# Expert routing tables built mostly by VectorE and evicted with tokens innermost, and the second layer's expert sums accumulated by tokens in four PSUM banks

## The chip, the cores and the metric

The kernel runs on one core of a Trainium2 chip. The metric is the device time of one execution in microseconds. TensorE does the matrix products into PSUM, VectorE and ScalarE the elementwise work and the copies out of PSUM, SyncE issues most transfers; GpSimd has little to do here.

## The reference

A model of two blocks. The first has two layers, each a mixer (a recurrent branch and a convolution, not touched here) and then `peer`, a layer of 16,384 small experts, for 512 tokens (256 of the sequence and 256 of a context) in the first layer and 256 in the second:

```python
s = jnp.einsum('thcd,hcnd->thcn', q, p['sub_keys'])        # 8 heads, two halves, 128 keys each
s1, i1 = lax.top_k(s[:, :, 0], PEER_TOPK); s2, i2 = lax.top_k(s[:, :, 1], PEER_TOPK)   # 16 of 128
...
best, pos = lax.top_k(cand, PEER_TOPK)                     # 16 of the 256 sums s1 + s2
eidx = jnp.take_along_axis(cidx, pos, axis=-1)             # expert = 128 * i1 + i2
gw = jax.nn.softmax(best, axis=-1)
u = jnp.take(p['peer_u'], eidx, axis=0)
act = jax.nn.gelu(jnp.einsum('td,thkd->thk', hc, u), approximate=False) * gw
v = jnp.take(p['peer_v'], eidx, axis=0)
return jnp.einsum('thk,thkd->td', act, v)
```

So each token takes 8 x 16 experts, with a weight each. After the second layer comes a norm, and then a second, dense block. All inputs and outputs are float32.

## The kernel before

The kernel gathers nothing. It computes all experts densely and multiplies by a routing table that is zero where a token did not choose the expert. The experts lie on a grid of 128 x 128; "an expert" below is one of 128 groups of 128 experts. Matrix operands are split into two parts (`whi`, `wlo` and the like: one cast by ScalarE, one subtraction by VectorE), and each product is made of three matmuls.

`peer` runs in two stages. **Stage 1**, `peer_route`, with the fills: for each block `b` of 128 tokens (four in the first layer, two in the second) VectorE finds the top-k (lines 1010 to 1014 for the most part), one-hot sums turn the result into indices, transposes put them into the rows `tr`, and `peer_table` builds the table. For every token it makes a 128 x 128 matrix as a product of two one-hot matrices: `qt` (VectorE, eight tokens at a time, line 1112) and `pt`, weighted by the gate. `pt` comes from VectorE in one instruction (line 1123) or from ScalarE in two, an `Abs` and a `Relu` (lines 1120, 1121). A matmul `wps` (line 1125, two records in the trace) makes one token; four tokens share a PSUM bank, and one ScalarE copy (line 1126) evicts them into `ws`, which holds 32 tokens and goes to DRAM as `wd`. There are four `pt` buffers, so one for each token of four.

Between these pieces `fill()` calls `gelu_u` ahead of time for 64 of the 128 experts: a transfer of weights, the split (lines 238, 240), 24 matmuls `s` (line 258), a Gelu on ScalarE (line 1136) and a store (`gd`). Fills that the table has left over run after it.

**Stage 2**, `peer_experts`: for groups of four experts it loads the table's part `wt`, multiplies it with the Gelu (line 1165), splits (lines 952, 953), and `products` (line 1180) sums the four experts' outputs in PSUM, channels on the partitions, tokens on the columns: 512 columns in the first layer, 256 in the second. `done` adds each sum to `x` on VectorE (line 1226). In the last group it also squares on ScalarE (lines 320, 322) and sums the squares with a matmul `nps` (line 324) for the norm that follows.

A scheduler decides at build time in which order instructions stand in each engine's queue, from priorities in the order of the code and from what it believes things cost. On the chip every engine goes through its queue in that order.

Of the kernel before, what the change touches and what calls it, by code (L numbers as in the profile page):

```python
# [11 lines left out]
F32 = mybir.dt.float32  # L12
# [10 lines left out]
P = 128  # L23
D = 1024
KO = 8
TX = 256
# [151 lines left out]
class Core:  # L178
# [924 lines left out]
    def peer_table(self, l, b, tr, wb, pp, wd, fill):  # L1103

        nc = self.nc
        iob = self.iota.unsqueeze(1).to_broadcast([P, 8, P])
        for g in range(b * 4, b * 4 + 4):
            ws = wb.tile([P, P, 32], F32, tag="ws", name="ws")
            for t0 in range(0, 32, 8):
                c0 = g * 32 + t0  # L1110
                qt = wb.tile([P, 8, P], F32, tag="qt", name="qt")
                nc.vector.tensor_tensor(qt, iob, tr[1][:, c0:c0 + 8].unsqueeze(2).to_broadcast([P, 8, P]),
                                        op=ALU.is_equal)
                for t1 in range(0, 8, 4):
                    ps = pp.tile([P, 4, P], F32, tag="mm", name="wps")
                    for t in range(4):
                        cs = slice(c0 + t1 + t, c0 + t1 + t + 1)
                        pt = wb.tile([P, P], F32, tag="pt", name="pt", bufs=4)
                        if t % 2:
                            nc.scalar.activation(pt, self.iota, AF.Abs, bias=tr[3][:, cs])  # L1120
                            nc.scalar.activation(pt, pt, AF.Relu, bias=tr[2][:, cs], scale=tr[4][:, cs])  # L1121
                        else:
                            nc.vector.tensor_scalar(pt, self.iota, tr[0][:, cs], tr[2][:, cs], op0=ALU.is_equal,
                                                    op1=ALU.mult)
                        nc.tensor.matmul(ps[:, t, :], pt, qt[:, t1 + t], start=True, stop=True)  # L1125
                    nc.scalar.copy(ws[:, :, t0 + t1:t0 + t1 + 4].rearrange("p i t -> p t i"), ps)  # L1126
            nc.sync.dma_start(wd[g], ws)
            fill(2 if g % 4 == 1 else 1)

# [9 lines left out]
    def peer_experts(self, l, T, h2, wd, gd, ge_pool, ps_s, ps_v, done):  # L1139

        nc, tc = self.nc, self.tc
        GI = 4
        TG = T // 32
        MB = 512 // T
        NV, NA = (GI + 1, GI + 2) if T == T2 else (2 * GI, 2 * GI)
        with tc.tile_pool(name="ep", bufs=2, reuse_waits="tile") as ep:
            def operands(g):
                wt = ep.tile([P, TG, GI, 32], F32, tag="wt", name="wt")
                nc.sync.dma_start(wt, wd[:, :, g * GI:g * GI + GI, :].rearrange("g p i t -> p g i t"))
                va, aa = [], []  # L1150
                for i in range(GI):
                    e = g * GI + i
                    if e in self.stash:
                        ge = ep.tile([P, T], F32, tag="gr", name="gr", bufs=2)
                        nc.sync.dma_start(ge, gd[self.stash.index(e)])
                    else:
                        ge = self.gelu_u(l, e, T, h2, ge_pool, ps_s)
                    raw = ep.tile([P, D], F32, tag="vraw", name="vraw", bufs=3)
                    nc.sync.dma_start(raw, self.A["pev"][l, e])
                    vl = ep.tile([P, D], F32R, tag="vl", name="vl", bufs=NV)  # L1160
                    vh = ep.tile([P, D], F32R, tag="vh", name="vh", bufs=NV)
                    self.split(vh, vl, raw)
                    va.append((vh, vl))
                    gv = ge[:, :T].rearrange("p (g t) -> p g t", t=32)
                    nc.vector.tensor_mul(gv, gv, wt[:, :, i, :])
                    ah = ep.tile([P, T], F32R, tag="ah", name="ah", bufs=NA)
                    al = ep.tile([P, T], F32R, tag="al", name="al", bufs=NA)
                    self.split(ah, al, ge[:, :T])
                    aa.append((ah, al))
                return va, aa  # L1170

            def products(g, va, aa):
                for m0 in range(0, KO, MB):
                    ps = ps_v.tile([P, MB, T], F32, tag="v", name="v")
                    for m in range(MB):
                        ms = slice((m0 + m) * P, (m0 + m) * P + P)
                        n = 0
                        for i in range(GI):
                            for wi, ai in ((0, 0), (0, 1), (1, 0)):
                                nc.tensor.matmul(ps[:, m, :], va[i][wi][:, ms], aa[i][ai], start=n == 0,  # L1180
                                                 stop=n == 3 * GI - 1)
                                n += 1
                    done(m0, ps, g == P // GI - 1)
            ops = operands(0)
            for g in range(P // GI):
                nxt = operands(g + 1) if T == TX and g + 1 < P // GI else None
                products(g, *ops)
                ops = nxt or (operands(g + 1) if g + 1 < P // GI else None)

    def peer(self, l, xin, xout):  # L1190
        nc, tc = self.nc, self.tc
# [572 lines left out]
```

## Time and profile before

| | |
|---|---|
| time, median of 3 runs | 5157.22 us (5154.08 to 5162.93) |
| profiled execution | 5154.13 us; span of its instructions 5152.3 us |
| busy: TensorE, VectorE, ScalarE | 4915.5 (95%), 3428.0 (67%), 2565.2 us (50%) |
| granted TensorE clock | 0.973 over the span, 1.00 in the first layer's table and in both expert stages |
| first layer, table (four blocks of 128 tokens) | 1262 to 1667 us |
| first layer, experts | from 1738 us |
| second layer, table (two blocks) | 3774 to 3995 us |
| second layer, experts | 4012 to 4562 us |

The busy time is an average over stages with different limits, so it is read stage by stage. Matmuls overlap one another: a matmul that lasts 0.28 us may be followed by the next one 0.12 us after its start, and a TensorE that looks busy may have gaps in its work.

### The profile page before, as it was taken

The page shows a single profiled execution, that of the slowest core. Times are in us where ns is not written, and L with a number is a line of the kernel's source. Part 1 is how long each engine was busy: PE and PEld are TensorE (multiplying, and loading weights), DVE is VectorE, ACT ScalarE, POOL GpSimd, SP SyncE. Part 2 cuts the span into 40 slices and gives each one's busy share as a digit, 9 for nine tenths or more (in the row PEclk, how much of TensorE's full clock was granted, in tenths as well). Part 3 has the DMA queues.
Part 4 walks back from the last instruction along what each step waited for, and adds up shares of the span by engine and source line. Part 5 has one row for each costly group of instructions (what it writes and reads, how often), then busy time and mean ns, then how long its engine had stood idle before and what let it go on. Part 6 is the DMA issues. An engine that isn't in the chain of part 4 may idle for free.

```text
span 5152.3 us, 85900 instructions
## 1 busy us (share of the span) xinstructions
PE 4915.5 (95%) x33106; PEld 4129.6 (80%) x33106; DVE 3428.0 (67%) x7590; ACT 2565.2 (50%) x4766; POOL 246.2 (5%) x629
## 2 busy tenths in 40 slices
PE   8999998999999999999999999998999999988889
PEld 6677776778777888888887787877989999987789
DVE  4788787558994455555555566666896777764654
ACT  4345444434988322222223455555588544465564
POOL 0111111000000000000000011211000000000000
PEclk9999999999999999999999899998999999999999
DMA  4332333533444644444442332324666877734444
GB/s 139 108 96 87 90 90 106 190 123 110 167 154 181 223 147 144 142 147 140 141 146 69 106 89 73 95 63 133 195 196 215 295 224 227 226 112 124 161 131 147
DMA packets 432973, 740.48 MB, mean 144 GB/s; under 512 B 132210, under 2 KB 273202, under 8 KB 427826
## 3 DMA queue, kind: packets, MB, share of 16 engines
q1 hardware_dynamic: 431042, 732.29, 45.4%
q8 instruction: 260, 4.26, 0.3%
q10 hardware_dynamic: 1520, 2.69, 0.2%
q14 instruction: 151, 1.24, 0.1%
HBM read 622.37 MB, written 112.49 MB: 143 GB/s over the span
## 4 chain that ended last, share of the span: by engine, by line
PE 73%; ACT 12%; DVE 9%; DMA 3%; issue 2%; POOL 0%; ACTq 0%; SPq 0%; DVEq 0%; POOLq 0%
PE v L1180 20%; PE s L258 14%; PE zps L258 5%; ACT ws L1126 3%; PE adaps L279 2%; PE gtps L258 2%; PE ops L258 2%; PE qps L258 2%; ACT pt L1121 2%; PE ops L1368 2%; DVE wlo L240 2%; ACT whi L238 2%; ACT pt L1120 2%; PE yp L558 1%; PE up L582 1%
## 5 line engine op out<-in xcount | busy, mean ns | idle before, releaser
L258 PE MATMUL s<-h,whi 128*128 128x512 f32 (+1 forms) x4096 | 1059.0, 343 | 1.3 <-ACT whi L238 0.7
L240 DVE TENSOR_TENSOR wlo<-wraw,whi 128x1024 fp32r<-128x1024 f32 (+2 forms) x602 | 724.8, 1206 | 470.1 <-ACT whi L238 460.4
L238 ACT CAST whi<-wraw 128x1024 fp32r<-128x1024 f32 (+2 forms) x602 | 622.1, 1035 | 725.5 <-PE s L258 191.7
L258 PEld LDWEIGHTS s<-h,whi 128*128 128x128 f32 x4096 | 704.1, 191 | 68.8 <-ACT ge L1136 1.0
L258 PE MATMUL s<-h,wlo 128*128 128x512 f32 (+1 forms) x2048 | 704.3, 344 | 9.3 <-DVE wlo L240 9.3
L1180 PE MATMUL v<-al,vh 128*128 128x512 f32 (+1 forms) x2048 | 689.7, 337 | 0.2 <-DVE al L953 0.2
L1180 PE MATMUL v<-ah,vl 128*128 128x512 f32 (+1 forms) x2048 | 689.7, 338 | 0.0
L1180 PE MATMUL v<-ah,vh 128*128 128x512 f32 (+1 forms) x2048 | 683.2, 338 | 1.5 <-ACT ah L952 1.0
L952 ACT CAST vh<-vraw 128x1024 fp32r<-128x1024 f32 x256 | 262.3, 1050 | 725.9 <-PE v L1180 574.1
L1226 DVE SCALAR_TENSOR_TENSOR x<-v,mod,x 128x256 f32<-128x256 f32 x768 | 334.0, 478 | 280.0 <-PE v L1180 279.9
L1180 PEld LDWEIGHTS v<-ah,vh 128*128 128x128 f32 x2048 | 387.3, 190 | 49.2 <-ACT ah L952 8.7
L258 PEld LDWEIGHTS s<-h,wlo 128*128 128x128 f32 x2048 | 390.4, 191 | 44.1 <-DVE wlo L240 10.3
L1180 PEld LDWEIGHTS v<-al,vh 128*128 128x128 f32 x2048 | 388.9, 190 | 45.8 <-DVE al L953 4.3
L1180 PEld LDWEIGHTS v<-ah,vl 128*128 128x128 f32 x2048 | 388.2, 190 | 40.6 <-issue 1.4
L953 DVE TENSOR_TENSOR vl<-vraw,vh 128x1024 fp32r<-128x1024 f32 x256 | 308.8, 1221 | 104.4 <-ACT vh L952 104.1
L258 PE MATMUL zps<-h,whi 128*128 128x512 f32 (+3 forms) x896 | 292.8, 404 | 18.9 <-DVE lz L363 7.5
L1125 PEld LDWEIGHTS wps<-qt,pt 128*128 128x128 f32 x1536 | 215.9, 190 | 109.5 <-ACT pt L1121 91.3
L1125 PE MATMUL wps<-qt,pt 128*128 128x128 f32 x1536 | 272.5, 292 | 22.1 <-ACT pt L1121 13.7
L258 PEld LDWEIGHTS zps<-h,whi 128*128 128x128 f32 (+1 forms) x896 | 167.6, 196 | 60.1 <-issue 19.4
L1126 ACT COPY ws<-wps 128x512 f32<-128x512 f32 x192 | 210.4, 1096 | 5.7 <-PE wps L1125 5.2
L279 PE MATMUL adaps<-adaw,cs 128*2 128x128 f32 x1536 | 205.7, 274 | 5.8 <-DMA adaw<-ada 4.4
L1121 ACT ACTIVATE pt<-pt,tr,tr 128x128 f32<-128x128 f32 x384 | 180.3, 489 | 2.5
(613 smaller groups left out, 9545.6 us busy)
## 6 DMA issues: line engine op xcount, KB each, us to landing
wraw<-peu SPq DMA_DIRECT2D x256, 512.0 KB, 4.0
vraw<-pev SPq DMA_DIRECT2D x256, 512.0 KB, 4.5
wraw<-win SPq DMA_DIRECT2D x139, 512.0 KB, 3.5
adaw<-ada SPq DMA_DIRECT2D x96, 512.0 KB, 3.6
wd<-ws SPq DMA_DIRECT2D x24, 2048.0 KB, 6.7
wt<-wd SPq DMA_DIRECT2D x32, 1024.0 KB, 6.8
wraw<-w_q SPq DMA_DIRECT2D x32, 512.0 KB, 3.7
gd<-ge SPq DMA_DIRECT2D x64, 256.0 KB, 2.3
```

What stands on the lines that cost most here:

```text
L238: nc.scalar.copy(hi, raw)
L240: nc.vector.tensor_sub(lo, raw, hi.bitcast(F32))
L258: nc.tensor.matmul(out, w[wi][:, k, :], a[ai][:, k, ts], start=n == 0, stop=n == 3 * ko - 1)
L279: nc.tensor.matmul(ps[0:2, i * P:i * P + P], self.cs[:, k, :], w[:, k, :], start=k == 0, stop=k == KO - 1)
L952: self.nc.scalar.copy(hi, src)
L953: self.nc.vector.tensor_sub(lo, src, hi.bitcast(F32))
L1120: nc.scalar.activation(pt, self.iota, AF.Abs, bias=tr[3][:, cs])
L1121: nc.scalar.activation(pt, pt, AF.Relu, bias=tr[2][:, cs], scale=tr[4][:, cs])
L1125: nc.tensor.matmul(ps[:, t, :], pt, qt[:, t1 + t], start=True, stop=True)
L1126: nc.scalar.copy(ws[:, :, t0 + t1:t0 + t1 + 4].rearrange("p i t -> p t i"), ps)
L1180: nc.tensor.matmul(ps[:, m, :], va[i][wi][:, ms], aa[i][ai], start=n == 0, stop=n == 3 * GI - 1)
L1226: nc.vector.scalar_tensor_tensor(x[:, k, ts], src[:, m, ts], self.mod[l][:, 40 + k, s:s + 1], x[:, k, ts], op0=ALU.mult, op1=ALU.add)
```

## The change

In `peer_table` ScalarE makes `pt` for one token of four instead of two, VectorE for three. The eviction's access patterns are turned: before it read PSUM in order and wrote each element 128 bytes from the last, now it reads four tokens 512 bytes apart and writes them next to each other. In the second layer (`T == TX`) `products_t` replaces `products`: the tokens' weighted activations are the stationary operand, 512 channels of the expert's output matrix the moving one, and the sums over all 128 experts stay in four PSUM banks (128 tokens x 512 channels each). At the end `channels` copies them out, transposes them 128 x 128 at a time, and hands them to `done`, which now runs once.

```diff
                     for t in range(4):
                         cs = slice(c0 + t1 + t, c0 + t1 + t + 1)
                         pt = wb.tile([P, P], F32, tag="pt", name="pt", bufs=4)
-                        if t % 2:
+                        if t == 3:
                             nc.scalar.activation(pt, self.iota, AF.Abs, bias=tr[3][:, cs])
                             nc.scalar.activation(pt, pt, AF.Relu, bias=tr[2][:, cs], scale=tr[4][:, cs])
                         else:
                             nc.vector.tensor_scalar(pt, self.iota, tr[0][:, cs], tr[2][:, cs], op0=ALU.is_equal,
                                                     op1=ALU.mult)
                         nc.tensor.matmul(ps[:, t, :], pt, qt[:, t1 + t], start=True, stop=True)
-                    nc.scalar.copy(ws[:, :, t0 + t1:t0 + t1 + 4].rearrange("p i t -> p t i"), ps)
+                    nc.scalar.copy(ws[:, :, t0 + t1:t0 + t1 + 4], ps.rearrange("p t i -> p i t"))
...
+            def products_t(g, va, aa):
+
+                for i in range(GI):
+                    for b in range(2):
+                        bs = slice(b * P, b * P + P)
+                        for n, (wi, ai) in enumerate(((0, 0), (1, 0), (0, 1))):
+                            for c in range(2):
+                                nc.tensor.matmul(acc[b][c], aa[i][ai][:, bs], va[i][wi][:, c * 512:c * 512 + 512],
+                                                 start=g + i + n == 0, stop=g == P // GI - 1 and i == GI - 1 and n == 2)
+
+            def channels():
+
+                rows = []
+                for b in range(2):
+                    r = ep.tile([P, D], F32, tag="vraw", name="vrow", bufs=3)
+                    for c in range(2):
+                        (nc.scalar.copy, nc.vector.tensor_copy)[c](r[:, c * 512:c * 512 + 512], acc[b][c])
+                    rows.append(r)
+                for m0 in range(0, KO, 2):
+                    ps = ps_s.tile([P, 2, T], F32, tag="s", name="vt")
+                    for m in range(2):
+                        for b in range(2):
+                            nc.tensor.transpose(ps[:, m, b * P:b * P + P], rows[b][:, (m0 + m) * P:(m0 + m) * P + P],
+                                                self.ident)
+                    done(m0, ps, True)
+            if T == TX:
+                acc = [[ps_v.tile([P, 512], F32, tag="v", name="acc") for c in range(2)] for b in range(2)]
+                products = products_t
```

The order in which the instructions stand changes in three regions alone: the two tables, and the second layer's expert stage.

ScalarE's queue in the last table block of the first layer (`L1120` is the `Abs`, `L1121` the `Relu`, `L1126` the eviction, `L1136` a fill's Gelu). Before:

```order
L1121 ACTIVATE pt<-pt,tr_9729,tr_9731 128x128
L1120 ACTIVATE pt<-iota,tr_9730 128x128
L1126 COPY ws<-wps 128x4x128
L1121 ACTIVATE pt<-pt,tr_9729,tr_9731 128x128
L1120 ACTIVATE pt<-iota,tr_9730 128x128
L1136 ACTIVATE ge<-s 128x512
L1121 ACTIVATE pt<-pt,tr_9729,tr_9731 128x128
L1120 ACTIVATE pt<-iota,tr_9730 128x128 x2
L1126 COPY ws<-wps 128x4x128
L1121 ACTIVATE pt<-pt,tr_9729,tr_9731 128x128 x2
```

and now, the same region:

```order
L1120 ACTIVATE pt<-iota,tr_9730 128x128
L1121 ACTIVATE pt<-pt,tr_9729,tr_9731 128x128
L1120 ACTIVATE pt<-iota,tr_9730 128x128
L1121 ACTIVATE pt<-pt,tr_9729,tr_9731 128x128
L1126 COPY ws<-wps 128x128x4
L1120 ACTIVATE pt<-iota,tr_9730 128x128
L1126 COPY ws<-wps 128x128x4
L1121 ACTIVATE pt<-pt,tr_9729,tr_9731 128x128
L1126 COPY ws<-wps 128x128x4
L1120 ACTIVATE pt<-iota,tr_9730 128x128
L1121 ACTIVATE pt<-pt,tr_9729,tr_9731 128x128
```

There is one `Abs` and one `Relu` to an eviction instead of two of each. The first eviction shown belongs to the quad of the first `Relu`, the second to that of the second `Relu`, the third to that of the `Relu` just ahead of it.

VectorE's queue in the same block (`L1123` makes a `pt`, `L1112` eight tokens of `qt`, `L240` is a fill's split). Before:

```order
L1123 TENSOR_SCALAR pt<-iota,tr_9727,tr_9729 128x128 x5
L1112 TENSOR_TENSOR qt<-iota,tr_9728 128x1024
L1123 TENSOR_SCALAR pt<-iota,tr_9727,tr_9729 128x128
L240 TENSOR_TENSOR wlo<-wraw,whi 128x1024
L1123 TENSOR_SCALAR pt<-iota,tr_9727,tr_9729 128x128 x2
L1112 TENSOR_TENSOR qt<-iota,tr_9728 128x1024
```

and now:

```order
L1123 TENSOR_SCALAR pt<-iota,tr_9727,tr_9729 128x128 x6
L1112 TENSOR_TENSOR qt<-iota,tr_9728 128x1024
L1123 TENSOR_SCALAR pt<-iota,tr_9727,tr_9729 128x128 x3
L240 TENSOR_TENSOR wlo<-wraw,whi 128x1024
L1123 TENSOR_SCALAR pt<-iota,tr_9727,tr_9729 128x128 x3
L1112 TENSOR_TENSOR qt<-iota,tr_9728 128x1024
```

Six instead of four `pt` stand to a `qt`. In this block 113 matmuls `s` now stand on TensorE between the table's matmuls instead of 188.

TensorE's queue at the end of the second layer's experts (`nps` is the norm, `pps` the dense block that follows). Before:

```order
L1180 MATMUL v<-ah,vh 128x256
L1180 MATMUL v<-al,vh 128x256
L1180 MATMUL v<-ah,vl 128x256
L324 MATMUL nps<-nsq,onesd 128x256 x4
L258 MATMUL pps<-hh_44317,whi 128x256 x2
```

and now:

```order
L1192 MATMUL acc<-vh,ah 128x512 x2
L1192 MATMUL acc<-vl,ah 128x512 x2
L1192 MATMUL acc<-vh,al 128x512 x2
L1207 MATMUL vt<-ident,vrow 128x128 x12
L324 MATMUL nps<-nsq,onesd 128x256 x12
L1207 MATMUL vt<-ident,vrow 128x128 x4
L324 MATMUL nps<-nsq,onesd 128x256 x4
```

Before, three more such groups of four `nps` stood among the last products; now all sixteen stand behind the last one, and the last four transposes behind twelve of them.

## Rows read from the trace of the kernel before

**Rows 1.** Windows: length, then busy us of each engine with its instructions, clock, DMA.

```profile
1262.00:1582.00 320.00, 309.41 (x1618) 236.86 (x1617) 278.55 (x762) 283.72 (x566) 0.00 (x0) 1.00 0.46 165
1582.00:1667.00 85.00, 83.11 (x449) 61.17 (x448) 45.33 (x84) 82.82 (x171) 0.00 (x0) 1.00 0.44 155
...
3774.00:3902.00 128.00, 121.95 (x962) 114.96 (x961) 109.96 (x227) 114.27 (x225) 0.00 (x0) 1.00 0.65 221
3902.00:3995.00 93.00, 88.72 (x673) 80.93 (x672) 55.40 (x93) 91.73 (x190) 0.00 (x0) 1.00 0.58 197
...
4012.00:4562.00 550.00, 548.34 (x4536) 546.06 (x4534) 413.63 (x697) 255.21 (x387) 1.50 (x1) 1.00 0.71 228
```

**Rows 2.** Windows of tile `s` alone: PE, PEld, DVE, ACT as above.

```profile
1262.00:1667.00 405.00, 310.77 (x1032) 178.28 (x1031) 0.00 (x0) 25.32 (x43) 1.00 0.46 163
1582.00:1667.00 85.00, 61.65 (x193) 32.00 (x192) 0.00 (x0) 4.68 (x8) 1.00 0.44 155
3774.00:3995.00 221.00, 168.59 (x1117) 142.75 (x1116) 0.00 (x0) 17.71 (x47) 1.00 0.62 211
```

**Rows 3.** Waits, 1582 to 1667: who, for whom, us in total, times, longest.

```profile
DVE pt L1123 <- PE wps L1125: 25.8, 34, 1.6
PEld wps L1125 <- ACT pt L1121: 16.8, 46, 0.7
```

**Rows 4.** Groups of instructions: count, busy us, mean ns, idle before.

```profile
L1126 ACT COPY ws<-wps 128x512 f32<-128x512 f32 x192 | 210.4, 1096 | 5.7 <-PE wps L1125 5.2
...
L1042 ACT COPY q<-qps 128x512 f32<-128x512 f32 x16 | 9.3, 581 | 0.0
```

**Rows 5.** Timeline in the first layer's tables: start, duration, instruction, idle before.

```profile
1405.92 0.60 DVE L1123 TENSOR_SCALAR pt<-iota,tr,tr 128x128 f32<-128x128 f32 x2
...
1407.30 0.87 ACT L1121 ACTIVATE pt<-pt,tr,tr 128x128 f32<-128x128 f32 x2
...
1408.07 0.39 ACT L1120 ACTIVATE pt<-iota,tr 128x128 f32<-128x128 f32 x1
...
1408.36 1.09 ACT L1126 COPY ws<-wps 128x512 f32<-128x512 f32 x1
1408.39 0.86 PE L1125 MATMUL wps<-qt,pt 128*128 128x128 f32 x6
...
1409.01 0.70 PE L258 MATMUL s<-h,whi 128*128 128x512 f32 x2
...
1665.61 0.39 ACT L1120 ACTIVATE pt<-iota,tr 128x128 f32<-128x128 f32 x1
1666.03 0.49 ACT L1121 ACTIVATE pt<-pt,tr,tr 128x128 f32<-128x128 f32 x1
1667.10 1.11 ACT L1126 COPY ws<-wps 128x512 f32<-128x512 f32 x1 [0.58 <-PE wps L1125]
1667.98 1.08 ACT L238 CAST whi<-wraw 128x1024 fp32r<-128x1024 f32 x1
```

**Rows 6.** Timeline of TensorE in both expert stages: 11th product after, 10th after.

```profile
4152.44 0.28 PE L1180 MATMUL v<-ah,vh 128*128 128x256 f32 x1
...
4153.76 0.28 PE L1180 MATMUL v<-ah,vl 128*128 128x256 f32 x1
2149.65 0.39 PE L1180 MATMUL v<-ah,vh 128*128 128x512 f32 x1
...
2151.91 0.39 PE L1180 MATMUL v<-al,vh 128*128 128x512 f32 x1
```

**Rows 7.** Timeline of TensorE at the second expert stage's end.

```profile
4548.19 1.99 PE L324 MATMUL nps<-nsq,onesd 128*128 128x256 f32 x8
4549.83 0.47 PE L1180 MATMUL v<-ah,vh 128*128 128x256 f32 x1
...
4561.30 0.28 PE L1180 MATMUL v<-ah,vl 128*128 128x256 f32 x1
4562.66 2.00 PE L324 MATMUL nps<-nsq,onesd 128*128 128x256 f32 x8 [1.09 <-ACT nsq L320]
```

More of the change, by code (lines that the diff above doesn't have):

```diff
@@ L1188, in peer_experts @@
                 ops = nxt or (operands(g + 1) if g + 1 < P // GI else None)
+            if T == TX:
+                channels()
     def peer(self, l, xin, xout):
```

## Prediction, made before the changed kernel ran

> **What bounds the kernel now.** I read the windows view first, cut at the places that the change touches. TensorE is busy 95 to 100% of each stretch [rows 1], but matmuls are pipelined, so I set the busy time against the work: counted records times their start-to-start time. A 512-column product follows the last one after 2.26/10 = 0.226 us, a 256-column one after 1.32/11 = 0.120 us [rows 6], and a table product (each `wps` matmul runs as two records) after 0.62/6 = 0.103 us per record [rows 5].
>
> - Second expert stage, 4012 to 4562: back to back, nothing waited for. TensorE is the bound and every nanosecond saved there is kept.
> - Last table block of layer 1, 1582 to 1667: TensorE's work is 193 x 0.226 + 256 x 0.103 = 70 of 85 us [rows 2]. ScalarE is busy 82.8 of 85, VectorE 45.3 [rows 1]; TensorE's longest waits end on `pt` of ScalarE (16.8 us), and VectorE waits 25.8 us for TensorE to hand `pt` buffers back [rows 3]. ScalarE is the bound. Layer 2's second block is alike, 91.7 of 93 us [rows 1].
> - First three blocks of layer 1, 1262 to 1582: VectorE 278.6, ScalarE 283.7 of 320 [rows 1], since VectorE also does the next block's top-k. Nearly balanced. Layer 2's first block, 110 and 114 of 128, likewise.
>
> Expert products `s` that the tables leave over run behind them at 0.226 or 0.120 us apiece. So what a table gains is gained only as TensorE's idle time inside it; leftover work is paid later.
>
> **Edit 1, one token in four on ScalarE.** ScalarE's price of four tokens before, start to start: two `Abs` at 0.29, two `Relu` at 0.385, the eviction 0.88 [rows 5], together 2.23. 32 quads make 71.4 us, and the remaining 11.4 of the 82.8 us are 8 fills (193/24), 1.4 each. After, by throughput: 0.29 + 0.385 + 0.88 = 1.56 a quad. But the order shows what throughput hides. Before, an `Abs` or a fill mostly stood between a `Relu` and the eviction that needs it. After, the eviction often stands right behind its own `Relu`, and ScalarE must wait out the way over TensorE: 1.07 us from `Relu`'s start to the eviction's, while `Abs` to `Relu` takes 0.42 (the last four rows of [rows 5]). The four `pt` buffers also make the next `Abs` wait for the same way. Walking the pattern of four quads in the order shown (Abs, Relu, Abs, Relu, evict, Abs, evict, Relu, evict, Abs, Relu, evict): 0, 0.42, 1.49, 1.91, 2.31, 3.19, 3.48, 4.36, 5.43, 6.31, 6.73, 7.80, and the next starts at 8.68. That is 2.17 us a quad with today's eviction: little won.
>
> **Edit 2, the eviction.** So its price decides. Today it reads PSUM in one run and writes SBUF in steps of 128 bytes: 1.096 us, against 0.581 for the copy of the same size without steps [rows 4]. After, it writes runs of four neighbours but reads PSUM in steps of 512 bytes, which no row shows. Bounds from the rows: 0.581 (start to start 0.38) and 1.096 (0.88); a dearer one is a rival. The write, the side that was stepped, is then packed by fours, so I put it nearer the row without steps: 0.8 us, 0.60 start to start. The same walk gives 7.63 per four quads, 1.91 each.
>
> Last block of layer 1: 32 x 1.91 = 61 plus some 4 us of fills that don't fit into the waits = 65, against 85: 20 less (12 less at 0.88, 27 less at the lower bound, where TensorE's 53 us of work and VectorE's 45 + 8 are the floor). But in the built order 365 instead of 316 `s` products are left over: 49 x 0.226 = 11 back.
> First three blocks: VectorE gets 96 more `pt`. One costs 0.34 alone, two take 0.60 [rows 5], so 0.26 to 0.34 each: 25 to 33 us on 278.6, 304 to 311. Of the 41 us that VectorE idled, I let 7 a block stay for the waits inside the table: 325 to 332 instead of 320, I take +6. The ends are 312 (-8) and 340 (+20).
> Layer 1 together: -20 + 11 + 6 = **-3** (-25 to +20).
>
> Layer 2, second block: 32 x 1.91 = 61, plus 14 fills of which half fit into waits, some 12: 73 against 93, -20; in the built order 84 products fewer stand inside and are paid later at 0.120: +10. First block: VectorE's 110 + 8 to 11, with some idle time, fills its 128 us; 0. **-10** (-16 to +3).
>
> **Edit 3, expert sums by tokens.** 3072 products of 256 columns become 1536 of 512, the columns are the same: 3072 x 0.120 = 368.6 against 1536 x 0.226 = 347.1, **-21.5**; the saving is the 14 ns by which two narrow products outlast a wide one, 1536 times. The 512-column rows are layer 1's, with the operands' roles swapped; both are full 128 x 128 loads, so I carry the price over. The VectorE updates that go bought nothing: it is busy 413.6 of 550 us there [rows 1] and isn't waited for.
> [...]
>
> New tail. Before, the norm of two channels stood in the stream of products three times, 1.64 us and a step of some 0.1 each, and its last part ended 3.4 us after the last product (4561.30 to 4564.66) [rows 7]. After, from the last product's start X: copies done at X+0.9 (0.3 as from `wps` to its eviction, 0.58 of copying), transposes and first update X+2.1, then twelve norm products, 0.41 apiece (8 records in 1.64 us), to X+7.5. The fourth group of transposes stands **behind** these twelve in TensorE's queue: its update and squares X+8.7, norm end about X+11.2. So 7.8 more at the end, 3 x 1.75 less inside: +2.5 (0 to +4). Experts: -21.5 + 2.5 = **-19** (-23 to -12).
>
> **Sum.** -3 - 10 - 19 = -32. The profiled execution took 5154.1 us (span 5152.3), 3 below the median of the runs; 5154 - 32 = **5122 us**. Ahead of the first table, between layer 1's experts and the second table, and behind the norm all instructions stand in the same order as before, so nothing else should move.
>
> **Rivals.**
> 1. The eviction stays at about 1.1 us. Layer 1's last block saves 12, layer 2's 12, the three blocks get longer by 10: layer 1 +9, layer 2 0, experts -19: 5144. For it: stepping nearly doubles the price in the one row there is. 0.18.
> 2. The other side: the stepped PSUM read is dearer than today's stepped write. ScalarE's chain runs through the eviction once a quad, in 64 quads where ScalarE binds and in half of the other 128: 13 us for every 0.1 us above 0.88. The 10 us left of rival 1 are used up at 0.96; slower by 0.2% from 1.04 start to start (about 1.26 us); at 1.5 it is 5225. For it: nothing measured; against: steps cost at most half a microsecond in the row there is. [...] 0.10.
> 3. Both tables run at TensorE's pace: idle falls from 405 - 1032 x 0.226 - 1024 x 0.103 = 66 to some 30 us in layer 1, in layer 2 from 221 - 1117 x 0.120 - 512 x 0.103 = 34 to 15 [rows 2]: -36 - 19 - 19, 5080. Against: the order's waits above. 0.10.
> 4. VectorE becomes the bound for good: 340 us in the three blocks, +20 - 12 + 11 in layer 1, -3 in layer 2, -19: 5151. 0.07.
> 5. [...] 0.05. [...]
>
> **Chances and range.** Forecast 0.50, its own range 5108 to 5134. For 8 in 10 the range goes from 5098 to 5153: it holds the forecast and rivals 1, 4 and 5, and leaves out 2 and 3. A difference of 0.2%, 10 us, is about what a measurement of this kernel can tell. Faster by more: forecast, 3, 5 and six tenths of 1, 0.76; same: the rest of 1, and 4, 0.14; slower: 2, 0.10.
>
> **What would show it.** Eviction: the mean of the `ws` copies, and whether ScalarE sits idle before them, waiting for `wps`. Last block of layer 1: some 65 us, ScalarE no longer 97% busy. Three blocks: VectorE above 90% busy. Experts: `acc` products 0.226 us apart and the stage some 531 us long; transposes twelve, then norms, then four. Wrong if the eviction costs more than 1.2 us, if `acc` products, which change PSUM bank each time, are not 0.226 apart, or if the three blocks take more than 340 us.

## The result, and the profile after

The changed kernel takes **5098.02 us** (median of 4 runs, 5095.33 to 5101.27) against 5155.65 for the kernel before (4 runs): ratio 0.9886, 95% interval 0.9869 to 0.9903. It is faster by 57.6 us where 32 were forecast, and lies at the very edge of the range. The profiled execution has a span of 5099.5 us, 52.9 less than before.

The windows view of the changed kernel, cut at the same places as [rows 1]: layer 1's first three blocks, its last block, layer 2's two blocks, layer 2's sums.

```profile
1263.90:1569.30 305.40, 300.03 (x1654) 249.94 (x1653) 300.32 (x862) 193.28 (x377) 0.00 (x0) 0.99 0.48 177
1569.30:1627.00 57.70, 57.70 (x366) 49.61 (x365) 47.76 (x112) 48.01 (x105) 0.00 (x0) 1.00 0.46 178
...
3741.80:3861.70 119.90, 118.23 (x959) 114.59 (x958) 116.54 (x259) 82.88 (x159) 0.00 (x0) 1.00 0.67 234
3861.70:3936.00 74.30, 74.15 (x596) 71.17 (x595) 58.59 (x122) 59.12 (x122) 0.00 (x0) 1.00 0.61 226
...
3959.00:4490.00 531.00, 527.46 (x3003) 466.34 (x3002) 320.38 (x440) 258.76 (x377) 2.03 (x2) 0.99 0.70 233
```

ScalarE, the fourth busy column, binds nowhere now: 193 of 305 us, 48 of 58. In the first three blocks VectorE is the busiest, with 300 of 305; whether it also sets their length is taken up in experiment 7. The groups view says why ScalarE is free; this is the eviction, with count, busy time, mean ns, and ScalarE's idle time before it:

```profile
L1126 ACT COPY ws<-wps 128x512 f32<-128x512 f32 x192 | 111.3, 580 | 48.7 <-PE wps L1125 45.9
```

It costs 0.580 us where it cost 1.096, and the copy without steps costs 0.581 [rows 4]. The idle time before it rose from 5.7 to 48.7 us: the wait behind its own `Relu` is there as the prediction had it, but on an engine with time to spare. The waits view of the last block has no long wait left (compare [rows 3]):

```profile
ACT ws L1126 <- PE wps L1125: 7.8, 13, 0.7
DVE pt L1123 <- PE wps L1125: 3.8, 11, 0.5
PEld wps L1125 <- ACT pt L1121: 2.8, 9, 0.3
```

TensorE's timeline in layer 2's sums shows two products per row, 0.45 to 0.46 us from row to row, so some 0.227 apiece, close to the 0.226 of the 512-column rows of [rows 6]:

```profile
4155.65 0.61 PE L1192 MATMUL acc<-vh,ah 128*128 128x512 f32 x2
4156.11 0.62 PE L1192 MATMUL acc<-vl,ah 128*128 128x512 f32 x2
4156.56 0.62 PE L1192 MATMUL acc<-vh,al 128*128 128x512 f32 x2
```

And the end of that stage, which answers to [rows 7]: the last product at 4489.79, twelve transposes, twelve norm products of two records, four transposes, four norm products, and then nothing until the dense block.

```profile
4490.02 1.81 PE L1207 MATMUL vt<-ident,vrow 128*128 128x128 f32 x12
...
4492.20 5.45 PE L324 MATMUL nps<-nsq,onesd 128*128 128x256 f32 x24 [0.37 <-ACT nsq L320]
...
4497.48 0.60 PE L1207 MATMUL vt<-ident,vrow 128*128 128x128 f32 x4
...
4499.11 1.99 PE L324 MATMUL nps<-nsq,onesd 128*128 128x256 f32 x8 [1.03 <-ACT nsq L320]
```

**Stages of all kernels.** Lengths in us, from first and last instructions in each trace: a block from its first `wps` to the next block's, the last block of a layer to the end of its last eviction; "left over" from there to the first expert product.

| | before | changed | again | sums alone | split alone | eviction alone | both table edits | split by place | no split |
|---|---|---|---|---|---|---|---|---|---|
| L1, three blocks | 320.4 | 304.1 | 303.8 | 320.5 | 331.5 | 294.2 | 304.0 | 294.3 | 294.3 |
| L1, last block | 85.7 | 58.9 | 58.9 | 85.7 | 69.2 | 76.0 | 58.9 | 62.0 | 76.0 |
| L1, left over | 70.4 | 82.0 | 82.0 | 70.3 | 81.5 | 70.9 | 82.0 | 85.1 | 70.9 |
| **L1 table, sum** | 476.5 | 445.0 | 444.7 | 476.5 | 482.2 | 441.1 | 444.8 | 441.4 | 441.1 |
| L2 table, left over with it | 237.8 | 217.4 | 217.3 | 237.8 | 234.2 | 216.9 | 217.4 | 216.7 | 218.7 |
| L2, sums | 549.3 | 530.7 | 528.8 | 526.2 | 554.6 | 550.0 | 554.7 | 526.0 | 523.5 |
| last product to dense block | 14.2 | 22.3 | 22.4 | 22.3 | 14.2 | 14.2 | 14.2 | 19.9 | 19.8 |
| dense block | 576.8 | 587.4 | 575.4 | 574.8 | 584.7 | 576.0 | 575.1 | 578.6 | 574.8 |

The parts of layer 1's table that kernels share repeat to a few tenths of a microsecond. Layer 2's sums do not (530.7, 528.8 and, with the same products in experiment 5, 526.0), nor does the dense block, which is a finding of its own.

### The profile page after: what moved, and what is told of

It reads as the page before. It is cut to its first block, busy times and chain, and to the rows that moved or that the text cites. A ratio compares the mean times of both kernels' runs of the same rounds, so it can differ in the third digit from the quotient of the medians.

```text
span 5099.5 us, 82466 instructions
## 1 busy us (share of the span) xinstructions
PE 4872.8 (96%) x31586; PEld 4065.7 (80%) x31586; DVE 3377.8 (66%) x7536; ACT 2388.0 (47%) x4384; POOL 246.9 (5%) x629
## 4 chain that ended last, share of the span: by engine, by line
PE 81%; DVE 9%; ACT 4%; DMA 4%; issue 1%; POOL 0%; SPq 0%; ACTq 0%; DVEq 0%; POOLq 0%
PE s L258 18%; PE v L1180 14%; PE acc L1192 6%; PE zps L258 5%; PE wps L1125 4%; PE adaps L279 3%; PE qps L258 2%; PE ops L258 2%; PE gtps L258 2%; PE ops L1399 2%; DVE wlo L240 2%; PE yp L558 1%; PE up L582 1%; PE zp L587 1%; PE zbps L258 1%
## 5 line engine op out<-in xcount | busy, mean ns | idle before, releaser
L240 DVE TENSOR_TENSOR wlo<-wraw,whi 128x1024 fp32r<-128x1024 f32 (+2 forms) x602 | 725.6, 1207 | 476.4 <-ACT whi L238 460.5
L1180 PE MATMUL v<-ah,vl 128*128 128x512 f32 x1024 | 401.3, 392 | 0.0
L1180 PE MATMUL v<-al,vh 128*128 128x512 f32 x1024 | 400.3, 391 | 0.0
L1180 PE MATMUL v<-ah,vh 128*128 128x512 f32 x1024 | 393.1, 391 | 0.5
L1257 DVE SCALAR_TENSOR_TENSOR x<-v,mod,x 128x256 f32<-128x256 f32 x512 | 220.0, 478 | 204.1 <-PE v L1180 204.1
L1125 PE MATMUL wps<-qt,pt 128*128 128x128 f32 x1536 | 229.6, 285 | 1.4 <-ACT pt L1121 0.6
L1180 PEld LDWEIGHTS v<-ah,vh 128*128 128x128 f32 x1024 | 191.0, 188 | 47.7 <-ACT ah L952 7.3
L1180 PEld LDWEIGHTS v<-al,vh 128*128 128x128 f32 x1024 | 192.2, 188 | 45.3 <-DVE al L953 4.0
L1180 PEld LDWEIGHTS v<-ah,vl 128*128 128x128 f32 x1024 | 192.2, 188 | 40.5 <-issue 1.4
L258 PEld LDWEIGHTS zps<-h,whi 128*128 128x128 f32 (+1 forms) x896 | 169.9, 198 | 60.8 <-issue 19.9
L258 PE MATMUL zps<-h,wlo 128*128 128x512 f32 (+3 forms) x448 | 179.2, 401 | 0.9 <-DVE wlo L240 0.9
L572 POOL COPY krp<-kr 64x128 f32<-64x128 f32 (+1 forms) x448 | 152.3, 340 | 549.2 <-PE yp L558 309.7
```

The costliest lines, as they stand in the source:

```text
L240: nc.vector.tensor_sub(lo, raw, hi.bitcast(F32))
L258: nc.tensor.matmul(out, w[wi][:, k, :], a[ai][:, k, ts], start=n == 0, stop=n == 3 * ko - 1)
L572: nc.gpsimd.tensor_copy(krp[hs, 0:n, hh], KR[d][hs, 0:n, c * 64:c * 64 + 64])
L1257: nc.vector.scalar_tensor_tensor(x[:, k, ts], src[:, m, ts], self.mod[l][:, 40 + k, s:s + 1], x[:, k, ts], op0=ALU.mult, op1=ALU.add)
```

## The experiments

**1. The sums alone.** The changed kernel with both table lines set back:

```diff
-                        if t == 3:
+                        if t % 2:
...
-                    nc.scalar.copy(ws[:, :, t0 + t1:t0 + t1 + 4], ps.rearrange("p t i -> p i t"))
+                    nc.scalar.copy(ws[:, :, t0 + t1:t0 + t1 + 4].rearrange("p i t -> p t i"), ps)
```

> The second layer's expert sums by tokens alone; both tables as before. First table to experts 476 us and second table to experts 297, as before. From the second layer's first expert product to the last: 549 less 1536 x 0.014 less three pauses of 1.75, 523 us; from the last product to the dense block 8 more than before (22 instead of 14). Theory 'the tail cools TensorE': the dense block behind it again takes 10 us more than before (587 instead of 577), so the time falls by 8 only, to about 5148. Theory 'each kernel meets the clock's falls at its own places': the dense block takes anything from 575 to 590, and the granted clock falls in another stretch of it; 5137 to 5150.

Measured: 5135.9 us, ratio 0.9959 (0.9945 to 0.9973). The sums took 526.2, 3 more than expected, and the way to the dense block 22.3. But the dense block took 574.8 us behind this longer tail: "the tail cools TensorE" fell. The other theory's bounds, 575 us for that block and 5137 for the whole, were missed by 0.2 and 1.1 us.

**2. The split alone.** The kernel before with `if t == 3:` in place of `if t % 2:`.

> One token in four on ScalarE, eviction as before, experts as before. Theory 'the eviction's price decides' (the walk of the prediction at 0.88 start to start gives 2.17 us a quad against 2.23 before, less what fits into waits): the last block of layer 1 takes 73 to 83 us instead of 85, the first three together 320 to 330 instead of 320, the time within 10 us of before. Theory 'the fewer activations decide' (throughput 1.56 a quad): last block 61, first three 305, layer 2's second block 70, the time 40 us below before.

Measured: 5164.0 us, ratio 1.0017 (1.0004 to 1.0030): no gain, if anything a loss. The three blocks took 331.5 us, 11.1 more than before, of which 26 more `s` products in them (867 instead of 841) make 5.9. The last block took 69.2 us, between what the two theories had, 73 to 83 and 61; of its 16.5 us less, 75 fewer `s` products (119 instead of 194) account for 17.0. Its windows (three blocks, last block):

```profile
1263.90:1595.40 331.50, 306.74 (x1646) 247.36 (x1645) 303.48 (x860) 225.97 (x375) 0.00 (x0) 1.00 0.46 163
1595.40:1664.60 69.20, 62.25 (x376) 50.54 (x375) 49.05 (x113) 60.74 (x107) 0.00 (x0) 1.00 0.41 151
```

and its waits in the three blocks, where TensorE waits for `pt` of ScalarE although ScalarE is busy only 226 of 331 us, and ScalarE for `wps`:

```profile
PEld wps L1125 <- ACT pt L1121: 45.9, 77, 1.0
ACT ws L1126 <- PE wps L1125: 25.0, 44, 1.3
PE wps L1125 <- ACT pt L1121: 19.6, 61, 0.5
```

That is the chain of the prediction's walk (an eviction of 1.1 us that waits behind its own `Relu`, and holds up the next `Abs`): a latency, which fewer activations did not shorten here.

**3. The eviction alone.** The kernel before with

```diff
-                    nc.scalar.copy(ws[:, :, t0 + t1:t0 + t1 + 4].rearrange("p i t -> p t i"), ps)
+                    nc.scalar.copy(ws[:, :, t0 + t1:t0 + t1 + 4], ps.rearrange("p t i -> p i t"))
```

> The eviction with tokens innermost alone; two tokens in four on ScalarE as before, experts as before. Theory 'the eviction's price decides': 0.58 us instead of 1.10, so ScalarE's quad is 2.23 - 0.50 = 1.73 us: last block of layer 1 some 69 us instead of 85, layer 2's second block 77 instead of 93; in the first three blocks VectorE keeps its 279 us of work, ScalarE falls to 234, and they take 290 to 300 instead of 320. Time 35 to 50 us below before. Theory 'the split decides': 10 us or less below before.

Measured: 5099.09 us, ratio 0.9901 (0.9880 to 0.9922). One line gives as much as the whole change, 57 us where 35 to 50 were expected; "the split decides" fell. Its eviction, and its windows (three blocks, last block):

```profile
L1126 ACT COPY ws<-wps 128x512 f32<-128x512 f32 x192 | 111.4, 580 | 10.4 <-PE wps L1125 7.7
```

```profile
1257.70:1551.90 294.20, 290.47 (x1619) 242.88 (x1618) 273.34 (x762) 249.98 (x566) 0.00 (x0) 1.00 0.50 179
1551.90:1627.90 76.00, 76.00 (x449) 63.27 (x448) 45.05 (x84) 73.10 (x172) 0.00 (x0) 1.00 0.49 174
```

The last block takes 7 us more than the 69 expected, though ScalarE works only 73 of 76: TensorE's work there, 192 products and 256 table products, is 69.8. Layer 2's second block was missed by as much (84.1 us, 77 expected).

**4. Both edits of the table.** The kernel before with the lines of 2 and 3.

> Both edits of the table, experts as before. First table to experts 445 us as in the changed kernel, second table to experts 275. Layer 2's experts 549 + 7 for the 58 products left over. Theory 'the parts add up': the time is before - 31 - 22 + 7 = 5109, and the dense block takes its 577 us, since the tail ahead of it is that of before. Theory 'each kernel meets the clock's falls at its own places': the dense block differs from 577 by more than 3 us, either way.

Measured: 5108.83 us, ratio 0.9911 (0.9895 to 0.9928), as added up. (The 275 us expected from the second table to the experts is not the stage of the table above, which has 217.4; the step from 297 to 275 is 22 us, the measured one 20.4.) Beside the eviction alone, the split makes the layer 1 table 3.7 us longer and layer 2's table with its sums 5.3 (217.4 + 554.7 against 216.9 + 550.0), against 9.7 between the medians, whose intervals overlap. The 3.7 us repeat: 444.7 to 445.3 in every kernel with both edits, 441.1 in experiments 3 and 9. The 5.3 are hardly more than the 4.7 by which layer 2's sums of the same products differ between executions. So behind a cheap eviction the split costs time in layer 1; for layer 2 that is not shown.

**5. The tail.** The changed kernel, with one group of transposes in a bank of the sums, which are free by then:

```diff
-                    ps = ps_s.tile([P, 2, T], F32, tag="s", name="vt")
+                    pool, tag = (ps_v, "v") if m0 == 6 else (ps_s, "s")
+                    ps = pool.tile([P, 2, T], F32, tag=tag, name="vt")
```

> The changed kernel, with the fourth group of transposes in a bank of the sums that the copies have freed, so that it need not stand behind the first twelve norm products. From the last product of the second layer's sums to the dense block: 22.27 us in the changed kernel. Theory 'the queue position of the fourth group costs': its update and squares no longer follow the twelve norm products, the norm is then paced by ScalarE's 16 pairs of squares at 0.41 us, and the stretch is 1.5 to 2 us shorter, 20.5. Theory 'the squares pace it anyway': under 0.5 us shorter. Everything ahead as in the changed kernel within 2 us.

Measured: 5079.67 us in one run, 19.86 us from the last product to the dense block, 2.4 less. All sixteen transposes now stand together, and the norm products run through:

```profile
4483.98 2.14 PE L1208 MATMUL vt<-ident,vrow 128*128 128x128 f32 x16
4486.17 7.17 PE L324 MATMUL nps<-nsq,onesd 128*128 128x256 f32 x32
```

The queue position did cost. The rest of the difference to 5098 is not the tail: the dense block (574.3) and the sums (526.0) were also shorter in this execution.

**6. Runs of two tokens.** The changed kernel, with its eviction in another order of writing:

```diff
-                    nc.scalar.copy(ws[:, :, t0 + t1:t0 + t1 + 4], ps.rearrange("p t i -> p i t"))
+                    nc.scalar.copy(ws[:, :, t0 + t1:t0 + t1 + 4].rearrange("p i (a t) -> p a i t", a=2), ps.rearrange("p (a t) i -> p a i t", a=2))
```

> The changed kernel, but its eviction writes runs of two tokens (8 bytes) instead of four (16 bytes): same 512 elements, same stepped read of PSUM. Measured so far: runs of one (4 bytes), PSUM read in one run, 1.096 us; runs of four, PSUM read stepped, 0.580; contiguous copy of the same size 0.581. [...] Theory 'anything below 16 bytes is slow': 1.1 us, last block 69 us.

Measured: 5109.42 us in one run, the stages of the table as in the changed kernel (three blocks 303.9, last block 59.1). The eviction:

```profile
L1126 ACT COPY ws<-wps 128x512 f32<-128x512 f32 x192 | 119.2, 621 | 47.7 <-PE wps L1125 45.6
```

So for the same 512 elements: runs of 4 bytes 1.096 us, of 8 bytes 0.621, of 16 bytes 0.580, no steps 0.581. "Anything below 16 bytes is slow" (1.1) fell. So does an even price for every run: by estimate, drawn from 512 runs at 1.096 us and 128 at 0.580, it puts these 256 at 0.75. The step from 4 to 8 bytes took off 0.475 us, that from 8 to 16 another 0.041; what makes the difference is not shown. The stepped read of PSUM, the fear of rival 2, costs nothing that these rows show (0.580 against 0.581).

**7. The split by place.** Two tokens in four on ScalarE, but one in layer 1's last block, with the sums and the tail of 5:

```diff
-                        if t == 3:
+                        if t == 3 or (t == 1 and (l or b < 3)):
```

> Eviction with tokens innermost, expert sums by tokens, the fourth group of transposes in a freed bank, and the split by place: two tokens in four on ScalarE, except in the last table block of layer 1, one in four. By adding the stages measured: first three blocks of layer 1 294 us (as with the eviction alone; 304 in the changed kernel), last block 59, first table to experts 436 (445 in the changed kernel), second table to experts 217, sums 527, tail 20.5. Time 15 to 20 below the changed kernel if the dense block takes the same 587 us there, about 5079; 5067 if it takes 575. Theory 'VectorE is the bound of the three blocks once the eviction is cheap': those 294 us. Theory 'TensorE or the chain over it is': the three blocks stay at 304.

Measured: 5076.54 us, ratio 0.9854 (0.9837 to 0.9870). The three blocks took 294.3 (VectorE has 273.6 us of work there instead of 300.3), the length that goes with "VectorE is the bound". Block by block the rows don't show such a bound. These are the third blocks of the changed kernel and of experiment 3, whose table there is that of this one:

```profile
1468.80:1568.00 99.20, 97.07 (x541) 81.33 (x540) 97.85 (x270) 61.85 (x122) 0.00 (x0) 1.00 0.49 178
1452.60:1551.90 99.30, 98.20 (x548) 82.07 (x547) 79.50 (x179) 83.59 (x190) 0.00 (x0) 1.00 0.51 180
```

Both take 99 us, with VectorE (the third busy column) at 97.9 or 79.5. All of the gain is in the second block, 110.7 to 100.3 us, where VectorE is busy nearly throughout in both but 33 fewer `s` products stand now. Over the three blocks 26 fewer products (841 instead of 867) make 5.9 of the 9.8 us; TensorE's idle time, counted as in the prediction, falls only from 29.1 to 25.1.

Nor does the table as a whole gain by it. It took 441.4, not 436: the last block's order left 63 more `s` products than experiment 3's to be paid behind it, 63 x 0.226 = 14.2 us, and they took what the shorter block (62.0 instead of 76.0) had given.

**8. The changed kernel again**, unaltered.

> The changed kernel once more, unaltered, for one question: is the fall of the granted clock 127 us into the dense block (0.50 for 18 us while TensorE is busy, with 10 us lost) a property of this kernel, or of one execution? Theory 'of the kernel': the dense block takes 587 us again with the fall in the same place. Theory 'of the execution': 575 to 578 us in some profiles and 587 in others. All stages ahead of it within 1 us of the first profile, the time 5095 to 5102.

Measured: 5095.15 us in one run; every stage from the first table to the end of layer 1's experts within half a microsecond, the mixer between the layers 980.3 instead of 973.8, the dense block 575.4 instead of 587.4. So it is of the execution, not of the kernel. The windows view over one and the same stretch of work, cut at the same instructions, first in the first profile of the changed kernel, then in this one (the last column but two is the granted clock):

```profile
4639.00:4668.00 29.00, 29.00 (x211) 23.90 (x208) 7.11 (x16) 7.53 (x18) 0.96 (x1) 0.71 0.22 69
```

```profile
4641.74:4663.74 22.00, 22.00 (x212) 18.18 (x208) 7.05 (x16) 7.55 (x18) 0.96 (x1) 1.00 0.32 91
```

29 us at a mean clock of 0.71 against 22 at 1.00. From 4640 to 4656 it was 0.50, from 4657 to the end of the stretch 1.00. In the 45 us ahead of the stretch TensorE was busy 40.3 us at a mean of 0.92, in it throughout; products of 32 to 64 columns alternate there with some of 256.

**9. No split.** As 7, with `if t % 2:` as in the kernel before, so that only the eviction, the sums and the tail differ from it.

> The changed kernel with the split of before everywhere (two tokens in four on ScalarE) and the fourth group of transposes in a freed bank; it differs from the last kernel only in the last table block of layer 1. There the eviction alone gave 75.9 + 70.9 us (block and products left over), the split by place 62.0 + 85.1. Theory 'behind a cheap eviction both tables go at TensorE's pace, and what a faster block leaves out is paid behind it': first table to experts 441 us as in both, the time that of the split by place within 3 us, 5074 to 5080. Theory 'the split is worth something where ScalarE binds': first table to experts 445 or more, the time 5 to 10 us above the split by place.

Measured: 5077.15 us, ratio 0.9846 (0.9827 to 0.9865), layer 1's table 441.1 us. It equals the split by place, so "worth something where ScalarE binds" fell. Its whole interval lies below that of the changed kernel, 0.9869 to 0.9903: it beats both kernels.

**10. Eight `pt` buffers.** As 9, with

```diff
-                        pt = wb.tile([P, P], F32, tag="pt", name="pt", bufs=4)
+                        pt = wb.tile([P, P], F32, tag="pt", name="pt", bufs=8)
```

> The kernel beside it with eight pt buffers instead of four. Of layer 1's first three blocks some 25 of 294 us are TensorE's idle time (294 less 841 products at 0.226 and 768 table products at 0.103). Theory 'pt comes late because its buffers come free late': with eight, VectorE and ScalarE run ahead, and the three blocks take 275 to 288 us. Theory 'VectorE's sum of work binds them' (it is busy 194 of the first two blocks' 195 us): the first two blocks stay at 94.6 and 100.3; only the third, where VectorE is busy 79.5 of 99.3, can shrink.

Measured: 5144.06 us in one run, layer 1's table 479.5, as long as before the change: the three blocks 103.4, 105.0 and 67.8, the last 113.6. Neither theory holds as it was put, since the scheduler answered the buffers with another order: `s` products left the first three blocks (673 instead of 841) for the last one (289 instead of 192). The waits view of that last block shows the engines handing work round in turn:

```profile
DVE wlo L240 <- ACT whi L238: 42.2, 9, 5.8
ACT whi L238 <- PE s L258: 27.4, 7, 4.0
DVE qt L1112 <- PE wps L1125: 19.4, 13, 2.3
```

Whether late buffers cost anything in the order with four is left open.

## Why the prediction was wrong

The direction was right, but the case that came is not the forecast's. By its own steps, in the profiled execution:

- **Layer 1's table: -3 forecast (-25 to +20), -31.5 measured.** This is the step that failed. *First three blocks*: +6 forecast, -16.3 measured. The sentence "Of the 41 us that VectorE idled, I let 7 a block stay for the waits inside the table" priced the 96 more `pt` and gave the cheaper eviction nothing, in blocks where ScalarE was busy 283.7 of 320 us [rows 1]. Taken apart, the split costs +11.1 there (331.5, inside the 325 to 332 of the prediction), the eviction gives 26.2 (294.2), both together 16.3. VectorE's work was sized well (300.3 and 303.5 against 304 to 311), but of its idle time, of which the prediction kept 21 us, 5 remain. That idle time was no fixed cost of the table: before the change VectorE waited 14.7 us for ScalarE's casts and 19.4 for `pt` buffers that TensorE hands back, and TensorE waited 53.2 us for ScalarE's `pt`, of which 13.4 are left (rows under this list). *Last block*: -20 forecast, -26.8 measured; *left over*: +11 and +11.6.
- **The eviction: 0.8 us chosen, 0.580 measured**, the lower of the two bounds. From its start to the next instruction it was not the 0.38 of the lower bound but 0.46 to 0.48. No row shows that 0.38: the unstepped copy has 0.48 in the trace of before, as the first two timeline rows under this list show. The walk through the queue came close at either price, without the fills that the prediction added to it: for the old eviction it gave 2.17 us a quad, 69.4 in 32, and experiment 2 measured 69.2; walked once more at 0.47 it gives 7.24 for four quads, 1.81 each, 57.9 in 32, against 58.9. The second agreement proves little, since TensorE's work in that block, 52.8 us, with 6 of idle time gives it too, and the block of experiment 7, with the same table work on ScalarE and 12 more `s` products (2.7 us), took 62.0.
- **Layer 2's table: -10 (-16 to +3), -17.2 measured**: -7.8 in the first block, where I had put 0 (the same omission), -20.6 in the second (forecast -20), +11.2 for 93 more products behind it (1656 instead of 1563, at 0.120; +10).
- **The sums: -19 (-23 to -12), -13.7 measured**: 18.6 less up to the last product and 8.0 more behind it, and 3.2 of the 93 products just named, which ran inside this stage, taken out. The wide product saves what [rows 6] promised: experiment 1's stage is 23.1 us shorter, of a forecast 21.5 for the products and 5.25 for the three pauses that go. The 3.6 us that are missing are nearly all one pause of TensorE early in the stage, from 4044.0 to 4047.3. The changed kernel has it too: 3.9 us for `whi`, in the waits from 3959 to 3980 shown under this list, where ScalarE waits for late weights ahead of it; just behind it the granted clock is 0.50, from 3971 to 3977. In experiment 5, with the same products, the pause was 1.6 us and the stage 4.7 us shorter; in experiment 9, with the products of experiment 1, it was 2.0 and the stage 25.8 us shorter than before. Rival 5, with 0.05 of the chances, had the wide product save far less than 21.5 us, from a price that no run shows; the runs show 0.227 us for a wide product where two narrow ones took 0.240 [rows 6], and the 23.1 us of experiment 1. It is out.

- **The tail: +7.8 at the end forecast, +8.0 measured**, by the position of the fourth group that the order showed; experiment 5 takes 2.4 of it back.
- **"Nothing else should move"**: +9.5 in the profiled execution, of which the dense block +10.6. Experiment 8 shows that this belongs to the execution. Without these 9.5 us the profiled execution would have taken 5091.8 us, below the range: that the time comes as near as it does is luck.

Waits in layer 1's first three blocks before (1262 to 1582), and the first of them in the changed kernel (1263.9 to 1569.3):

```profile
PEld wps L1125 <- ACT pt L1121: 53.2, 132, 1.0
DVE pt L1123 <- PE wps L1125: 19.4, 43, 1.6
DVE wlo L240 <- ACT whi L238: 14.7, 11, 4.2
...
PEld wps L1125 <- ACT pt L1121: 13.4, 47, 0.3
```

The timeline of the kernel before, a copy without steps and the instruction right behind it, and that of the changed kernel, the eviction and the instruction right behind it:

```profile
1126.42 0.58 ACT L1042 COPY q<-qps 128x512 f32<-128x512 f32 x1
1126.90 0.77 ACT L1034 COPY sc<-sps 128x128 f32<-128x128 f32 x4
...
1590.80 0.57 ACT L1126 COPY ws<-wps 128x512 f32<-128x512 f32 x1
...
1591.26 0.40 ACT L1120 ACTIVATE pt<-iota,tr 128x128 f32<-128x128 f32 x1
```

Its waits at the start of layer 2's sums, 3959 to 3980:

```profile
PEld s L258 <- ACT whi L238: 3.9, 1, 3.9
DVE vl L953 <- ACT vh L952: 3.9, 5, 2.4
ACT vh L952 <- DMA vraw<-pev: 3.8, 3, 2.8
```

**The rivals.** Rival 3, TensorE's pace, priced at 5080 with a chance of 0.10, is the one that came nearest: TensorE's idle time by the same formula is 363.0 - 984 x 0.226 - 1024 x 0.103 = 35 us in layer 1 (rival: some 30, before: 66) and 194.3 - 1036 x 0.120 - 52.7 = 17 in layer 2 (rival: 15, before: 34). I held the order's waits against it; they exist (48.7 us before the evictions), but with the eviction at 0.58 they no longer end last. Block by block of layer 1 that idle time is 15 to 20 us with the dear eviction (the kernel before, experiment 2) and 6 to 12 with the cheap one (the changed kernel, experiments 3 and 7), whichever engine makes `pt`. Rival 1, the dear eviction, is what experiment 2 measures: layer 1's table +5.7 where it had +9. Rival 2 had the wrong sign of the risk: the stepped read of PSUM was free (0.580 us against 0.581). Rival 4 had VectorE busy throughout the three blocks, and it is, 300 of 305 us, but at 305 and not 340, and by the third block of experiment 7 it is not shown to be their bound.

**The edit named first was worth nothing.** Of the 57.6 us, the eviction and the sums give all; the split takes 3.7 back in layer 1's table, and 7.6 of the whole when it stands alone. A block that it shortens hands `s` products to the stretches beside it. The parts do not add up to the whole: both table edits (47.6) and the sums (20.5) make 68.1 us. The profiled execution lost 10.6 in the dense block, but experiment 8, which did not, took 5095.15 us against the median of 5098.02, so where the 10 us go is open.

## What to carry to other kernels

Two edits to one chain are not priced one after the other: a cheaper eviction paid as much where another engine looked as busy (7.5 to 9.5 us in each of the first three blocks) as where ScalarE alone did (9.7 in the last), because the other engine's idle time was waiting, directly or by way of TensorE, for ScalarE. Where a stage's filler work is paid later at TensorE's pace, ask what TensorE waits for and not who is busiest, and try each edit alone before keeping the set. Compare kernels stage by stage when single stages differ by 10 us from one execution to the next, as the dense block did here (587.4 and 575.4).

## What the hardware showed that was not expected

- Of three run lengths, a ScalarE copy with a stepped write paid dearly only for runs of one 4-byte element: 1.096 us, against 0.621 for two and 0.580 for four, and the PSUM read in steps of 512 bytes added nothing (0.580 against 0.581).
- The granted clock fell to 0.50 in a stretch of the dense block in one execution and stayed at 1.00 there in another of the same kernel, with TensorE recorded as busy throughout; the block took 587.4 and 575.4 us. Over the 14 runs beside experiments 1 to 4 the kernel before ranged from 5146.91 to 5172.11.
